# RMSNorm: a one-row store placed between the first and second tile's loads, the third tile in 64 KB rows, gamma in two pieces

## The chip, the cores and the metric

The kernel runs on one core of a Trainium2 chip. Times are device microseconds of that core; unless a span is named, a time is the median of several executions. All executions used here are fast (one core, granted clock 1.0). "Queue" below means the queue of transfers that SyncE issues; every transfer of the kernel is spread over 16 DMA engines, each of which moves its own share.

## The reference

```python
def reference(x, gamma):          # x: 16 x 1024 x 512 float32, gamma: 512 float32
    eps = 1e-5
    rms = np.sqrt(np.mean(x ** 2, axis=-1, keepdims=True) + eps)
    return (x / rms * gamma).astype(np.float32)
```

33.6 MB are read and as many written, with little arithmetic per byte.

## The kernel before

The 16,384 rows form four tiles (t) of 128 partitions x 32 rows x 512 floats: one partition of a tile is 64 KB, contiguous in HBM. Three buffers (slots) hold them; tile 3 reuses the buffer of tile 0. The text says tile 0 to tile 3; the change's own words call tile 2 the third. Rows are handled in groups of 8: ScalarE squares and sums (in every second group VectorE does the summing), VectorE multiplies each row by its 1/rms and by gamma, in place.

```python
    load(0, 0, 0, 8)
    load(0, 0, 8, 16)
    load(0, 0, 16, 32)
    load(1, 1, 0, 32)

    gamma_row = const.tile([1, D], fp32)
    nc.scalar.dma_start(out=gamma_row, in_=gamma.unsqueeze(0))
    # ... gamma is spread over the partitions by a matmul; row_stats and apply are cut

    def transfers(t, g):              # called after apply of tile t, rows g to g+8
        if (t, g) == (0, 0):
            store(0, 0, 0, 1)
            load(2, 2, 0, 16)
            store(0, 0, 1, 2)
            load(2, 2, 16, 24)
            store(0, 0, 2, 3)
            load(2, 2, 24, 32)
        elif (t, g) == (0, 24):
            store(0, 0, 3, 32)
        elif (t, g) == (1, 8):
            store(1, 1, 0, 16)
            load(3, 0, 0, 16)
            load(3, 0, 16, 32)
        # ... stores of tile 1, 2 and 3 in the same way, cut
```

`load(t, slot, r0, r1)` and `store(...)` each issue one transfer of 128 partitions on SyncE, which issues in order and waits for what a transfer needs.

Of the kernel before, what the change touches and what calls it, by code (L numbers as in the profile page):

```python
# [1 line left out]

# [4 lines left out]


@with_exitstack
def kernel(  # L10
    ctx: ExitStack,
    tc: tile.TileContext,
    x: bass.AP,
    gamma: bass.AP,
    out: bass.AP,
):
    nc = tc.nc
    P = nc.NUM_PARTITIONS
    eps = 1e-5
    fp32 = mybir.dt.float32  # L20
    AF = mybir.ActivationFunctionType
    OP = mybir.AluOpType

    xf = x.flatten_outer_dims()
    of = out.flatten_outer_dims()
    N, D = xf.shape
    R = 32
    G = 8
    H = 4
    assert N == 4 * P * R  # L30

    xv = xf.rearrange("(t p r) d -> t p r d", p=P, r=R)
    ov = of.rearrange("(t p r) d -> t p r d", p=P, r=R)

    const = ctx.enter_context(tc.tile_pool(name="const", bufs=1))
    stats = ctx.enter_context(tc.tile_pool(name="stats", bufs=4))
    psum = ctx.enter_context(tc.tile_pool(name="psum", bufs=2, space=bass.MemoryType.PSUM))

    slots = [const.tile([P, R, D], fp32, name=f"slot{i}") for i in range(3)]

    def load(t, slot, r0, r1):
        nc.sync.dma_start(out=slots[slot][:, r0:r1], in_=xv[t][:, r0:r1])

    def store(t, slot, r0, r1):
        nc.sync.dma_start(out=ov[t][:, r0:r1], in_=slots[slot][:, r0:r1])

    load(0, 0, 0, 8)
    load(0, 0, 8, 16)
    load(0, 0, 16, 32)
    load(1, 1, 0, 32)  # L50

    gamma_row = const.tile([1, D], fp32)
    nc.scalar.dma_start(out=gamma_row, in_=gamma.unsqueeze(0))
    ones_col = const.tile([1, P], fp32)
    nc.vector.memset(ones_col, 1.0)  # L55
    gamma_psum = psum.tile([P, H, D], fp32, name="sq")
    nc.tensor.matmul(gamma_psum[:, 0], ones_col, gamma_row, start=True, stop=True)  # L57
    gamma_b = const.tile([P, D], fp32)
    nc.vector.tensor_copy(out=gamma_b, in_=gamma_psum[:, 0])  # L59

    eps_t = const.tile([P, 1], fp32)
    nc.vector.memset(eps_t, eps)  # L62
    sq_scratch = const.tile([P, D], fp32)

    def row_stats(slot, g):
        ss = stats.tile([P, G], fp32, name="ss")
        rms = stats.tile([P, G], fp32, name="rms")
        rstd = stats.tile([P, G], fp32, name="rstd")
        if (g // G) % 2:
            for h in range(0, G, H):  # L70
                sq = psum.tile([P, H, D], fp32, name="sq")
                nc.scalar.activation(out=sq, in_=slots[slot][:, g + h : g + h + H, :], func=AF.Square)  # L72
                nc.vector.tensor_reduce(  # L73
                    out=ss[:, h : h + H], in_=sq, axis=mybir.AxisListType.X, op=OP.add
                )
        else:
            for r in range(G):
                nc.scalar.activation(  # L78
                    out=sq_scratch,
                    in_=slots[slot][:, g + r, :],  # L80
                    func=AF.Square,
                    accum_out=ss[:, r : r + 1],
                )
        nc.scalar.activation(out=rms, in_=ss, func=AF.Sqrt, bias=eps_t, scale=1.0 / D)  # L84
        nc.vector.reciprocal(out=rstd, in_=rms)  # L85
        return rstd

    def apply(slot, g, rstd):
        for r in range(G):
            nc.vector.scalar_tensor_tensor(  # L90
                out=slots[slot][:, g + r, :],
                in0=slots[slot][:, g + r, :],
                scalar=rstd[:, r : r + 1],
                in1=gamma_b,
                op0=OP.mult,
                op1=OP.mult,
            )

    groups = [(t, g) for t in range(4) for g in range(0, R, G)]
    slot_of = [0, 1, 2, 0]  # L100

    def transfers(t, g):
        if (t, g) == (0, 0):
            store(0, 0, 0, 1)
            load(2, 2, 0, 16)
            store(0, 0, 1, 2)
            load(2, 2, 16, 24)
            store(0, 0, 2, 3)
            load(2, 2, 24, 32)
        elif (t, g) == (0, 24):  # L110
            store(0, 0, 3, 32)
        elif (t, g) == (1, 8):
            store(1, 1, 0, 16)
            load(3, 0, 0, 16)
            load(3, 0, 16, 32)
        elif (t, g) == (1, 24):
            store(1, 1, 16, 32)
        elif (t, g) == (2, 24):
            store(2, 2, 0, 32)
        elif (t, g) == (3, 8):  # L120
            store(3, 0, 0, 16)
        elif (t, g) == (3, 24):
            store(3, 0, 16, 32)

    ahead = row_stats(0, 0)
    for k, (t, g) in enumerate(groups):
        rstd = ahead
        if k + 1 < len(groups):
            tn, gn = groups[k + 1]
            ahead = row_stats(slot_of[tn], gn)  # L130
        apply(slot_of[t], g, rstd)
        transfers(t, g)


# [1 line left out]
_INS = ['x', 'gamma']  # L136
_OUTS = [((16, 1024, 512), 'float32')]


# [23 lines left out]
```

## Time and profile before

| | before |
|---|---|
| time, median of the first 3 runs | 162.5 us (162.17 to 163.0) |
| span in the profile | 160.3 us |
| data queue, share of 16 engines' span | 97.8% |
| VectorE / ScalarE busy | 76% / 50% |
| first data packet / last packet on any engine (packet records) | 1.74 / 158.97 us |

From the page of the kernel before: busy time, then the queue (packets, MB, share of 16 engines' span), then the bytes, then the chain of work that ended last, by engine. (PE and PEld are TensorE, DVE is VectorE, ACT ScalarE, POOL GpSimd; SPq marks what SyncE issues, L45 is line 45 of the kernel.)

```profile
span 160.3 us, 415 instructions
PE 2.0 (1%) x2; PEld 0.5 (0%) x2; DVE 122.6 (76%) x163; ACT 80.1 (50%) x162; POOL 0.2 (0%) x4
...
q1 hardware_dynamic: 2592, 67.11, 97.8%
...
HBM read 33.56 MB, written 33.55 MB: 419 GB/s over the span
...
DVE 69%; ACT 12%; DMA 4%; issue 2%; DVEq 0%
```

The queue is full nearly all the time, so the kernel ends when the bytes have passed. Next, SyncE's issues in order of time (start, length, what; a merged line spans several issues and the wait between them).

```profile
0.73 1.89 SPq L42 DMA_DIRECT2D slot<-in_x_dram  x4
20.54 0.35 SPq L45 DMA_DIRECT2D out_dram<-slot  x1
20.93 0.43 SPq L42 DMA_DIRECT2D slot<-in_x_dram  x1
21.41 0.43 SPq L45 DMA_DIRECT2D out_dram<-slot  x1
...
45.84 23.22 SPq L45 DMA_DIRECT2D out_dram<-slot  x2
```

All of tiles 0 and 1 is issued by 2.6 us; when the first small store is issued at 20.54 us, tile 1 still lies ahead of it in the queue, 19 us of work. ScalarE's first instruction on tile 1, with its idle time and what ended it:

```profile
42.16 0.63 ACT L78 ACTIVATE sq_scratch<-slot 128x512 f32<-128x512 f32 x1 [6.91 <-DMA slot<-in_x_dram]
```

### The profile page before, as it was taken

The page shows a single profiled execution, that of the slowest core. Times are in us where ns is not written, and L with a number is a line of the kernel's source. Part 1 is how long each engine was busy: PE and PEld are TensorE (multiplying, and loading weights), DVE is VectorE, ACT ScalarE, POOL GpSimd, SP SyncE. Part 2 cuts the span into 40 slices and gives each one's busy share as a digit, 9 for nine tenths or more (in the row PEclk, how much of TensorE's full clock was granted, in tenths as well). Part 3 has the DMA queues.
Part 4 walks back from the last instruction along what each step waited for, and adds up shares of the span by engine and source line. Part 5 has one row for each costly group of instructions (what it writes and reads, how often), then busy time and mean ns, then how long its engine had stood idle before and what let it go on. Part 6 is the DMA issues. An engine that isn't in the chain of part 4 may idle for free.

```text
span 160.3 us, 415 instructions
## 1 busy us (share of the span) xinstructions
PE 2.0 (1%) x2; PEld 0.5 (0%) x2; DVE 122.6 (76%) x163; ACT 80.1 (50%) x162; POOL 0.2 (0%) x4
## 2 busy tenths in 40 slices
PE   4000000000000000000000000000000000000000
PEld 1000000000000000000000000000000000000000
DVE  0102999999995199999999999999999999950000
ACT  3099739900499999969009600796099400000000
POOL 0000000000000000000000000000000000000000
DMA  6999999969799999998899999999999799799993
GB/s 197 437 413 523 392 392 523 523 262 523 327 403 407 456 435 503 474 444 356 385 441 466 401 409 490 401 401 499 409 515 474 327 507 458 335 392 450 458 401 139
DMA packets 2597, 67.13 MB, mean 419 GB/s; under 512 B 290, under 2 KB 290, under 8 KB 675
## 3 DMA queue, kind: packets, MB, share of 16 engines
q1 hardware_dynamic: 2592, 67.11, 97.8%
q14 instruction: 3, 0.02, 0.0%
q10 hardware_dynamic: 2, 0.00, 0.0%
HBM read 33.56 MB, written 33.55 MB: 419 GB/s over the span
## 4 chain that ended last, share of the span: by engine, by line
DVE 69%; ACT 12%; DMA 4%; issue 2%; DVEq 0%
DVE slot L90 51%; DVE ss L73 17%; ACT sq_scratch L78 7%; ACT sq L72 4%; DMA slot<-in_x_dram 4%; DVE rstd L85 1%; ACT rms L84 1%; DVEq L158 0%
## 5 line engine op out<-in xcount | busy, mean ns | idle before, releaser
L90 DVE SCALAR_TENSOR_TENSOR slot<-slot,rstd,gamma_b 128x512 f32<-128x512 f32 x128 | 85.7, 738 | 0.1
L78 ACT ACTIVATE sq_scratch<-slot 128x512 f32<-128x512 f32 x64 | 40.0, 625 | 16.0 <-DMA slot<-in_x_dram 14.7
L73 DVE TENSOR_REDUCE ss<-sq 128x4 f32<-128x2048 f32 x16 | 36.0, 2274 | 10.1 <-ACT sq L72 10.0
L72 ACT ACTIVATE sq<-slot 128x2048 f32<-128x2048 f32 x16 | 29.8, 1862 | 8.1 <-DVE ss L73 8.1
L84 ACT ACTIVATE rms<-ss,eps_t 128x8 f32<-128x8 f32 x16 | 4.6, 298 | 26.6 <-DVE ss L73 26.4
L78 ACT ACTIVATION_READ_ACCUMULATOR sq_scratch<-slot 128x1 f32 x64 | 11.9, 187 | 0.0
L85 DVE RECIPROCAL rstd<-rms 128x8 f32<-128x8 f32 x16 | 3.1, 192 | 5.7 <-ACT rms L84 5.7
L59 DVE COPY gamma_b<-sq 128x512 f32<-128x512 f32 x1 | 0.7, 692 | 3.2 <-PE sq L57 3.2
L57 PE MATMUL sq<-gamma_row,ones_col 1*128 1x512 f32 x2 | 2.0, 1122 | 2.1 <-DMA gamma_row<-in_gamma_dram 2.1
L78 ACT ACT_TABLE_LOAD x1 | 1.3, 1283 | 1.3 <-PEq L147 1.3
L84 ACT ACT_TABLE_LOAD x1 | 1.3, 1283 | 0.0
L55 DVE MEMSET ones_col<- 1x128 f32 x1 | 0.2, 165 | 0.8 <-PEq L147 0.8
L57 PEld LDWEIGHTS sq<-gamma_row,ones_col 1*128 1x128 f32 x2 | 0.5, 306 | 2.1 <-issue 2.1
L147 POOL MEMSET const-bfloat16-1.0<- 128x1 bf16 x1 | 0.1, 101 | 0.0
L147 POOL MEMSET const-uint8-127<- 128x1 uint8 x1 | 0.1, 101 | 0.0
L147 POOL MEMSET const-float32-0.0<- 128x1 f32 x1 | 0.1, 98 | 0.2 <-issue 0.2
L147 POOL MEMSET const-float32-1.0<- 128x1 f32 x1 | 0.1, 98 | 0.0
L62 DVE MEMSET eps_t<- 128x1 f32 x1 | 0.1, 59 | 0.0
## 6 DMA issues: line engine op xcount, KB each, us to landing
slot<-in_x_dram SPq DMA_DIRECT2D x4, 4096.0 KB, 24.7
out_dram<-slot SPq DMA_DIRECT2D x4, 4096.0 KB, 22.5
slot<-in_x_dram SPq DMA_DIRECT2D x4, 2048.0 KB, 11.5
out_dram<-slot SPq DMA_DIRECT2D x1, 7424.0 KB, 35.8
out_dram<-slot SPq DMA_DIRECT2D x3, 256.0 KB, 32.1
gamma_row<-in_gamma_dram ACTq DMA_DIRECT2D x1, 2.0 KB
slot<-in_x_dram SPq DMA_DIRECT2D x1, 40.0
out_dram<-slot SPq DMA_DIRECT2D x1
```

The lines of the kernel that those rows point to most:

```text
L55: nc.vector.memset(ones_col, 1.0)
L57: nc.tensor.matmul(gamma_psum[:, 0], ones_col, gamma_row, start=True, stop=True)
L59: nc.vector.tensor_copy(out=gamma_b, in_=gamma_psum[:, 0])
L62: nc.vector.memset(eps_t, eps)
L72: nc.scalar.activation(out=sq, in_=slots[slot][:, g + h : g + h + H, :], func=AF.Square)
L73: nc.vector.tensor_reduce(out=ss[:, h : h + H], in_=sq, axis=mybir.AxisListType.X, op=OP.add)
L78: nc.scalar.activation(out=sq_scratch, in_=slots[slot][:, g + r, :], func=AF.Square, accum_out=ss[:, r : r + 1],)
L84: nc.scalar.activation(out=rms, in_=ss, func=AF.Sqrt, bias=eps_t, scale=1.0 / D)
L85: nc.vector.reciprocal(out=rstd, in_=rms)
L90: nc.vector.scalar_tensor_tensor(out=slots[slot][:, g + r, :], in0=slots[slot][:, g + r, :], scalar=rstd[:, r : r + 1], in1=gamma_b, op0=O ...
L147: nc = _bacc.Bacc("TRN2", target_bir_lowering=False, num_devices=1)
```

## The change

The intent: fewer and larger transfers. Two of the three one-row stores go, the third tile (tile 2) is one load with 64 KB per partition instead of three, gamma is loaded in two pieces, and the load of tile 1 moves behind the remaining one-row store.

```diff
     load(0, 0, 16, 32)
-    load(1, 1, 0, 32)
 
     gamma_row = const.tile([1, D], fp32)
-    nc.scalar.dma_start(out=gamma_row, in_=gamma.unsqueeze(0))
+    cuts = [D * i // 2 for i in range(3)]
+    for a, b in zip(cuts, cuts[1:]):
+        nc.scalar.dma_start(out=gamma_row[:, a:b], in_=gamma.unsqueeze(0)[:, a:b])
@@ transfers
             store(0, 0, 0, 1)
-            load(2, 2, 0, 16)
-            store(0, 0, 1, 2)
-            load(2, 2, 16, 24)
-            store(0, 0, 2, 3)
-            load(2, 2, 24, 32)
+            load(1, 1, 0, 32)
+            load(2, 2, 0, 32)
         elif (t, g) == (0, 24):
-            store(0, 0, 3, 32)
+            store(0, 0, 1, 32)
```

## The prediction

> **What bounds the kernel now.** The transfers. The page's queue section gives the data queue 97.8% of 16 engines' span and 419 GB/s; VectorE is busy 76%. In the packet records under that view, from the first data packet (1.74 us) to the last semaphore packet (158.96 us), the 16 engines together are idle for the equal of only about 0.6 us, nearly all at the two ends. The chain of waits names VectorE for 69%, but VectorE finishes at 142.5 us and the last store's packets only come up at 148 us, behind older ones. So a saving counts only if it shortens the queue's work, and a delay costs only if the queue runs dry. The Trainium skill, "DMA: Bandwidth & Descriptors", Bandwidth, gives a ceiling of 435 GB/s; 64 KB packets here took 2.418 us, 27.1 bytes/ns on one engine, 434 GB/s on 16: the trace agrees.
>
> **What the change does to the queue's work.** A packet of 2 KB takes 84 ns, 16 KB 611, 32 KB 1213, 64 KB 2418. Consecutive packets overlap by about 4 ns, so each extra packet costs about 4.7 ns. Per partition, two 2 KB store packets join the large store and the third tile's 32+16+16 KB become one 64 KB: four packets less, 32 per engine, 0.15 us. Four transfers less drop four 9 ns semaphore packets per engine, 0.02 us. Load-to-store turns fall from five to three; the last load packets before a turn ran longer by about 0.34 us at the first store (39 us) and 0.04 to 0.1 us later. Two later ones saved are worth about 0.1 us. Together about 0.25 us.
>
> **What it moves.** The second tile's load is issued behind the first small store. The timeline shows that store issued at 20.54 us, after the first VectorE row; its issue takes about 0.4 us, so the load goes out near 20.95. Tile 0's last packets end between 21.73 and 22.03 us. Issue to first packet took 1.0 us at the kernel's start, so the store's packets are ready near 21.55 us, eight of 80 ns per engine fill until about 22.4 to 22.7, and the load's are ready near 22.0. The queue should just not run dry; slack is 0.2 us for the store, 0.4 us for the load. I allow 0.1 us for a partial gap. Nothing ahead of that row changes order on ScalarE or VectorE.
>
> Tile 1 lands about 0.65 us later (its compute began at 42.16). That is off the path: the large store is issued with some 16 us of queue ahead, tile 1's first store with 11, the last store at 142.5 with 5.6. Tile 2 lands 1 to 2 us earlier, which nobody waits for. Gamma's second issue takes 0.5 us on ScalarE's queue, while ScalarE idles until 7.88.
>
> **Prediction.** 162.5 - 0.25 + 0.1: 162.3 us, range 161.7 to 163.0. Faster by over 2%: 0.01; within 2%: 0.97; slower: 0.02.
>
> **What would show it.** Data packets 2016 against 2592. The one-row store begins between 21.6 and 22.1 us, tile 1's 64 KB packets near 22.5, hardly any idle time around 20 to 24 us; ScalarE's wait for tile 1 ends near 42.8; VectorE ends at 142 to 143.5.
>
> **What would make it wrong.** A longer delay from issue to first packet: every us beyond 1.2 goes straight into the total, as all later transfers wait behind. Or a first row later than 20.5 us. The spread of 0.8 us exceeds the effect.

## The result

| | before | changed |
|---|---|---|
| time, median of 6 runs | 162.45 us (162.17 to 163.0) | 164.94 us (164.4 to 165.26) |
| ratio, 95% interval | | 1.0149 (1.0123 to 1.0174) |
| last packet of the 16 engines (packet records) | 157.82 to 158.97 us | 12 engines 159.36 to 160.22, 4 engines 161.6 to 161.93 us |

Ratios here and below are the mean time of one kernel's fast runs over that of the other's in the same rounds, so not quite the ratio of the medians quoted. By the 2% measure the time is the same; by the interval it is 1.5% slower. 164.94 us lies outside the predicted 161.7 to 163.0.

The page of the changed kernel, the same parts, and the first line of its chain that ended last:

```profile
span 163.1 us, 408 instructions
PE 2.0 (1%) x2; PEld 0.5 (0%) x2; DVE 122.8 (75%) x163; ACT 80.0 (49%) x162; POOL 0.2 (0%) x4
...
q1 hardware_dynamic: 2016, 67.11, 96.9%
...
HBM read 33.56 MB, written 33.55 MB: 411 GB/s over the span
...
DVE 52%; DMA 19%; ACT 15%; issue 2%; DVEq 0%; SPq 0%
```

Packets fell exactly as counted ahead, from 2592 to 2016, and still the queue's share fell and the span grew. The part of DMA in the chain went from 4% to 19%. SyncE's issues:

```profile
0.73 1.33 SPq L42 DMA_DIRECT2D slot<-in_x_dram  x3
20.75 0.35 SPq L45 DMA_DIRECT2D out_dram<-slot  x1
21.14 0.94 SPq L42 DMA_DIRECT2D slot<-in_x_dram  x2
46.06 25.92 SPq L45 DMA_DIRECT2D out_dram<-slot  x2
```

and ScalarE's first instruction on tile 1:

```profile
45.52 0.63 ACT L79 ACTIVATE sq_scratch<-slot 128x512 f32<-128x512 f32 x1 [10.06 <-DMA slot<-in_x_dram]
```

In the chain that ended last (start, length, what) of the changed kernel, tile 1's load now stands by itself:

```profile
20.64 0.21 DVE rstd L86
20.85 0.25 SPq L45
21.10 0.04 issue
21.14 24.36 DMA slot<-in_x_dram
45.50 0.02 issue
```

Tile 1 is issued at 21.14 us, as foreseen to 0.2 us, and ScalarE gets it at 45.52 us, where 42.8 was predicted. A 64 KB row takes 2.418 us on its engine and each engine carries eight, 19.3 us. So 24.36 us from issue to landing leaves about 5 us for something else. The records of single packets show what:

```
tile 1's first 64 KB packet on each of the 16 engines, start in us (changed kernel)
22.69 22.79 22.98 22.99 23.00 23.05 23.06 23.07 23.09 23.12 23.14 23.18 | 24.59 24.71 24.90 25.14
end of tile 0's last packets: 21.61 to 22.24; one-row store's packets: from 21.79 to 23.18
```

Twelve engines pass from the store to tile 1 without a gap. Four finish the store among the first, at 22.70 to 22.89 us, find nothing, and stand idle for about 2 us. (The records do not name the engine; which packets follow each other is read from their times. On the twelve a 64 KB packet starts within 6 ns of the end of the store's last semaphore packet, the 4-byte packet by which an engine reports its share done; on the four none does.) In addition the packets are slower around this place: the store's 2 KB packets took up to 204 ns instead of 84, and the first two 64 KB packets of an engine up to 3.35 us instead of 2.418. The four engines stay behind the others to the end: they finish tile 1 at 44.7 to 45.2 us while the others finish at 42.9 to 43.5, and close the kernel 1.4 to 2.6 us after them. Each engine has a fixed share of the partitions, so the others cannot help. The Trainium skill, "DMA: Bandwidth & Descriptors", The descriptor swizzle, gives that fixed assignment; this trace is consistent with it, though its records name no engine: in tile 1's load and in all nine later transfers the group of four ends at least 1.1 us after the slowest of the twelve.

Three quantities per engine describe the loss (averages over 16 engines, worked out from the packet records: idle from 20 to 30 us; stretch, that is packet time above the usual 84, 611, 1213, 2418 ns of its size, or above size over 27.1 bytes/ns for other sizes):

| | before | changed |
|---|---|---|
| idle, 20 to 30 us | 0.00 us | 0.62 us (about 2 us on four engines) |
| stretch, 20 to 30 us | 0.01 us | 0.98 us |
| stretch, 30 to 56 us | 0.37 us | 0.05 us |
| stretch, 56 to 66 us (turn to the large store of tile 0) | 0.15 us | 1.08 us |
| median engine's last packet | 158.05 us | 159.86 us |

The median engine loses 1.8 us, mostly by stretch; the last engine, which ends the kernel, loses about 3 us in this pair of profiles.

### The profile page after: what moved, and what is told of

Same layout as the page of the kernel before. It is cut to its first block, busy times and chain, and to the rows that moved or that the text cites. A ratio compares the mean times of both kernels' runs of the same rounds, so it can differ in the third digit from the quotient of the medians.

```text
span 163.1 us, 408 instructions
## 1 busy us (share of the span) xinstructions
PE 2.0 (1%) x2; PEld 0.5 (0%) x2; DVE 122.8 (75%) x163; ACT 80.0 (49%) x162; POOL 0.2 (0%) x4
## 3 DMA queue, kind: packets, MB, share of 16 engines
q1 hardware_dynamic: 2016, 67.11, 96.9%
## 4 chain that ended last, share of the span: by engine, by line
DVE 52%; DMA 19%; ACT 15%; issue 2%; DVEq 0%; SPq 0%
DVE slot L91 38%; DMA slot<-in_x_dram 19%; DVE ss L74 13%; ACT sq_scratch L79 8%; ACT sq L73 6%; DVE rstd L86 1%; ACT rms L85 0%; DVEq L156 0%; SPq L45 0%
```

## The experiments

The first four were to settle which part of the change costs. Theory D: the queue runs dry because tile 1's load comes too late. Rivals: G, the second gamma piece; P, 64 KB packets next to a turn between loading and storing.

**a1_gamma_one**, gamma in one piece again.

```diff
-    cuts = [D * i // 2 for i in range(3)]
-    for a, b in zip(cuts, cuts[1:]):
-        nc.scalar.dma_start(out=gamma_row[:, a:b], in_=gamma.unsqueeze(0)[:, a:b])
+    nc.scalar.dma_start(out=gamma_row, in_=gamma.unsqueeze(0))
```

> Undoes gamma in two pieces, all else as changed. Theory D (the queue runs dry when the second tile's load is issued only behind the one-row store): unchanged, 164.9 us +-0.5, four or more engines again start tile 1's 64 KB packets about 2 us after their last store packet. Rival G (the second gamma piece, which landed only at 6.5 us, disturbs the start): back to 162.3 to 162.7 us.

Measured: 165.12 us (before on the same chip 162.65), ratio 1.0155 (1.0129 to 1.0182). Three engines start tile 1 late, at 23.8, 24.0 and 24.7 us. D had said four or more. G falls: gamma is not it.

**a2_load1_first**, tile 1 loaded up front again, all else changed.

```diff
     load(0, 0, 16, 32)
+    load(1, 1, 0, 32)
@@ transfers
             store(0, 0, 0, 1)
-            load(1, 1, 0, 32)
             load(2, 2, 0, 32)
```

> Undoes the late load alone: tile 1's load issued up front as before, then one one-row store, tile 3's rows of 64 KB, gamma in two. Theory D: the late engines vanish; 162.2 to 163.3 us, since one cost is left, the stretched 64 KB packets of tile 2 at the turn to the large store (0.97 us per engine after, against about 0.5 us for all turns of before). Rival P (64 KB packets next to a turn between loads and stores are the main cost, not the late load): stays at 164.0 or above. Rival G: stays near 164.9.

Measured: 162.24 us against 162.65, ratio 0.9972 (0.9955 to 0.9988). No idle time from 20 to 30 us. Its span is 160.7 us, and its first instruction on tile 1 is back where it was in the kernel before:

```profile
42.14 0.63 ACT L80 ACTIVATE sq_scratch<-slot 128x512 f32<-128x512 f32 x1 [6.74 <-DMA slot<-in_x_dram]
```

D holds: putting this one load back takes the whole loss away, and what is left of the change is a small gain. P as the main cost falls.

**a3_tile2_halves**, the third tile in two loads of 32 KB rows.

```diff
-            load(2, 2, 0, 32)
+            load(2, 2, 0, 16)
+            load(2, 2, 16, 32)
```

> As changed, but the third tile in two loads of 32 KB rows. Theory D says the late start is the same, so at least 163.8 us. Rival P, for the second stretch: the last packets of tile 2 before the large store near 61 us lose their stretch (from 0.97 us mean per engine to under 0.2 us) and the time falls by 0.6 to 0.9 us, to about 164.1. If packet size does not matter at the turn: 164.9 and the stretch stays near 1 us in total.

Measured: 165.21 us, ratio 1.0161 (1.0135 to 1.0187); the stretch from 56 to 66 us is 1.12 us, as with 64 KB rows (1.08). P falls for the second stretch too: the row size is not its cause.

**a4_quarter_first**, eight rows of tile 1 up front, the rest behind the store.

```diff
     load(0, 0, 16, 32)
+    load(1, 1, 0, 8)
@@ transfers
             store(0, 0, 0, 1)
-            load(1, 1, 0, 32)
+            load(1, 1, 8, 32)
```

> As changed, but 8 rows of tile 1 (4.9 us of queue) are loaded up front and 24 rows after the one-row store, so the queue is not dry when the store and the load come. Theory D: no engine idles near 22 to 25 us, time 162.3 to 163.5 us. Rival (it is the place of the store between loads, not the dry queue): stays near 164.5 or above.

Measured: 162.29 us, ratio 0.9975 (0.9960 to 0.9990), idle from 20 to 30 us 0.01 us. The store may stand between loads; the queue only must not be nearly empty then. This settles the first question.

The second question is why a load issued 0.5 to 1.1 us before tile 0's last packets end, with 0.65 us of store packets besides, comes too late. Theory L: under load the way from issue to first packet is long on some engines. Rival R: an engine that once finds its queue empty takes 2 us to restart. Rival S: the turn from load to small store and back costs. Later B: the small store just ahead delays the load. The next kernels vary the lead. Where a load is to be held back without a store, one column of its buffer is first written by VectorE from a finished row; the load overwrites it, so results stay correct.

**b1_cushion1**, one row of tile 1 (0.65 us of queue) up front; **b2_cushion2**, two rows; **e1_cushion4**, four rows.

```diff
     load(0, 0, 16, 32)
+    load(1, 1, 0, n)          # n = 1, 2, 4
@@ transfers
-            load(1, 1, 0, 32)
+            load(1, 1, n, 32)
```

> As changed, but one row of tile 1 (8 packets, about 0.65 us of queue per engine) is loaded up front. Theory L (a load issued while the queue is busy reaches some engines only up to 4 us after its issue, whatever they do meanwhile): the late engines still start tile 1's large packets near 24 to 25 us, idle about 1.3 us instead of 2, so 163.7 to 164.6 us. Theory R (a queue found empty for even a moment takes 2 us to restart): the descriptors are in time and no engine is late, 162.2 to 162.8 us.

> The same with two rows up front (about 1.3 us of queue). Theory L: late engines idle about 0.7 us, 163.0 to 163.8 us, between the one-row cushion and none. Theory R: 162.2 to 162.8 us, the same as the one-row cushion.

> As changed, with four rows of tile 1 (about 2.4 us of queue per engine) loaded up front. Theory L: the worst start seen was 4.0 us after the issue, 2.0 us after the queue ran dry, so 2.4 us of lead just covers it: no late engine, 162.2 to 162.7 us, level with eight rows (162.29) and clearly under two rows (163.07). If eight rows were needed for another reason: 162.8 or more.

Measured, with the two ends of the series (stretch and idle from each one's profile):

| rows of tile 1 up front | time | ratio to before | idle 20-30 us | stretch 20-30 / 56-66 us |
|---|---|---|---|---|
| 0 (changed) | 164.94 | 1.0149 | 0.62 | 0.98 / 1.08 |
| 1 | 164.09 | 1.0104 | 0.18 | 0.30 / 1.34 |
| 2 | 163.07 | 1.0036 | 0.05 | 0.48 / 0.33 |
| 4 | 161.83 | 0.9973 | 0.02 | 0.33 / 0.91 |
| 8 | 162.29 | 0.9975 | 0.01 | 0.28 / 0.70 |
| 32 (a2_load1_first) | 162.24 | 0.9972 | 0.00 | 0.00 / 0.55 |

The medians come from several sets of runs, so compare the ratios. (The 161.83 us with four rows is below the 162.2 to 162.7 expected, on a chip on which the kernel before was at 162.31.) The instruction of ScalarE that waited for the rest of tile 1, with one, two and four rows in front:

```profile
44.29 0.63 ACT L80 ACTIVATE sq_scratch<-slot 128x512 f32<-128x512 f32 x1 [8.92 <-DMA slot<-in_x_dram]
```

```profile
43.27 0.63 ACT L80 ACTIVATE sq_scratch<-slot 128x512 f32<-128x512 f32 x1 [7.33 <-DMA slot<-in_x_dram]
```

```profile
42.86 0.63 ACT L80 ACTIVATE sq_scratch<-slot 128x512 f32<-128x512 f32 x1 [5.43 <-DMA slot<-in_x_dram]
```

The time falls row by row and is level from four rows on, 2.4 us of lead. Counted from the issue of the rest of tile 1 to its first packet, the work ahead was 1.9 us with one row, 2.8 with two and 4.2 with four; only the last exceeds the 4.0 us that the slowest engine of the changed kernel took. R, which wanted one row to suffice, falls. L had the times of one and two rows right, but its picture of the engines was not. With one row a single engine stands out, 3.20 us after the issue where the others start within 2.66. For two rows it foresaw late engines idle for 0.7 us, and the profile shows 0.05 us of idle time on average and 0.48 us of stretch. These two profiles are not typical of their kernels either: the one-row profile is its slowest run (164.97 us), the two-row profile its fastest (162.69).

**b3_held_row7**, the loads held until eight rows are multiplied, so that the queue is truly empty.

```diff
     def apply(...):           # for the first group only, after row 7
+                for s in (1, 2):
+                    nc.vector.tensor_copy(out=slots[s][:, 0, 0:1], in_=slots[0][:, g + r, 0:1])
```

> As changed, but tile 1's and tile 2's loads are held until the eighth row is multiplied (a one-column copy into their buffers, overwritten by the load), so they are issued near 25.6 us into a queue that has been empty since about 23. If the latency is long only under load (L), all 16 engines start tile 1 between 26.6 and 27.3 us, 1.0 to 1.6 us after the issue as at the start of the kernel, with no late group, and the time is about 4.2 us over the version with the load up front: 166 to 167 us. If restarting an empty queue costs 2 us or more (R), starts lie at 27.6 us or later and the time is 167.3 or more.

Measured: 168.06 us, ratio 1.0348 (1.0321 to 1.0375). SyncE's issues:

```profile
20.62 0.35 SPq L45 DMA_DIRECT2D out_dram<-slot  x1
26.05 0.80 SPq L42 DMA_DIRECT2D slot<-in_x_dram  x2
```

and the queue's line of its page, 94.7% where the changed kernel had 96.9%:

```profile
q1 hardware_dynamic: 2016, 67.11, 94.7%
```

All 16 engines start tile 1 between 27.02 and 27.35 us, 0.97 to 1.30 us after the issue. So an empty queue restarts in about 1 us on every engine, and R falls a second time. But the time is 168.06, above L's 166 to 167: beyond 4.5 us of idle, the first packets after the empty time are stretched by 0.77 us per engine, and those near the turn to the large store by 1.03. L had no term for that. It is to be seen at the kernel's own start: there the packets that start before 2.0 us took 0.53 us longer per engine than later ones in the profile of before, and 0.25 to 0.58 us in the others.

**c1_held_nostore**, no small store, the loads held to the same moment as in the changed kernel.

```diff
+                for s in (1, 2):       # after row 0 of the first group
+                    nc.vector.tensor_copy(out=slots[s][:, 0, 0:1], in_=slots[0][:, g + r, 0:1])
@@ transfers
-            store(0, 0, 0, 1)
             load(1, 1, 0, 32)
             load(2, 2, 0, 32)
         elif (t, g) == (0, 24):
-            store(0, 0, 1, 32)
+            store(0, 0, 0, 32)
```

> No one-row store at all; tile 1's and tile 2's loads are held to about the same moment (the first row multiplied, 20.9 us) by a one-column copy. L or R: some engines still start tile 1 late, idle 2 us or more since there is no store to bridge, 164.5 to 166 us. Rival S (the turn from a load to a small store and back is what costs): no late engine, 162.3 to 163 us.

Measured: 164.13 us, ratio 1.0109 (1.0078 to 1.0140). The issue:

```profile
20.80 0.80 SPq L42 DMA_DIRECT2D slot<-in_x_dram  x2
```

Tile 1 starts 1.15 to 1.96 us after its issue at 20.80 us. Both expectations miss in part: no group of engines starts 2 us after the rest, as S said, yet the time is nowhere near 162.3 to 163. The loss here is 0.38 us of idle and 0.76 plus 1.23 us of stretch. A load issued as the queue runs out costs without any store in front of it; the store makes the worst engine later still.

**c2_all_held**, the one-row store too is held (row 0 is multiplied last of its eight), then the loads, all into an empty queue.

```diff
-        for r in range(G):
+        for r in [*range(1, G), 0] if first else range(G):
@@ and the same one-column copies after row 0
```

> Row 0 is multiplied last of its eight, so the one-row store is issued near 25.5 us and the loads near 26.2 us, both into an empty queue. If it is the busy queue that makes the second issue late (L): all engines start tile 1's packets within 1.6 us of the load's issue, as in the held run without a store in front (0.97 to 1.30 us), time within 0.5 us of that run's 168.06. If it is the small store just ahead (B, descriptors of a transfer are made only after those of the one before): some engines start 2 to 4 us after the issue, a late group is there at the end, and the time is 169 us or more.

Measured: 168.39 us, ratio 1.0348 (1.0331 to 1.0364). The issues:

```profile
25.45 0.35 SPq L45 DMA_DIRECT2D out_dram<-slot  x1
26.18 0.82 SPq L42 DMA_DIRECT2D slot<-in_x_dram  x2
```

The store's first packets come 0.85 us after its issue at 25.45 us; tile 1's, issued at 26.18 us, 0.99 to 1.36 us after on thirteen engines, and 1.81, 1.82 and 2.10 us after on three. Between the two expectations: the store ahead delays a few engines by up to 0.8 us even when the queue is empty (some of B), but not to the 4 us of the changed kernel, and the time is within 0.5 us of the previous held run (L).

**c3_store_on_act**, the one-row store issued from ScalarE's queue, the loads held to the same moment as in c1_held_nostore.

```diff
-            store(0, 0, 0, 1)
+            nc.scalar.dma_start(out=ov[0][:, 0:1], in_=slots[0][:, 0:1])
@@ and the same one-column copies after row 0
```

> As changed, with the one-row store issued from ScalarE's queue and the loads held to the same moment on the other. B says the two still hinder each other: late engines (2 us or more after the issue), 164.3 to 165.2. If only the order within one queue matters: load starts as in the held run without a store (1.2 to 2.0 us after issue) and 163.8 to 164.3 us. No version of this is expected to beat the kernel before.

Measured: 164.06 us, ratio 1.0087 (1.0062 to 1.0111). Tile 1 starts 1.13 to 2.66 us after its issue at 20.85 us. In time it is level with the held run without a store; two engines, at 2.07 and 2.66 us, are later than any there (1.96). The other queue mends nothing, and it does not keep the two apart: on thirteen engines one 2 KB packet of the store now passes per 64 KB packet of tile 1, so that the store's packets, done by 23.2 us in the changed kernel, end only at 38.5 us. This kernel is therefore not a clean test of B.

Start of tile 1's large packets after its issue, first and last engine, over all these runs:

| run | queue at the issue | store issued just ahead | first / last engine |
|---|---|---|---|
| b3_held_row7 | empty | no | 0.97 / 1.30 us |
| c2_all_held | empty but for the store | yes | 0.99 / 2.10 us |
| c1_held_nostore | busy to about 1 us after | no | 1.15 / 1.96 us |
| c3_store_on_act | the same | on the other queue | 1.13 / 2.66 us |
| changed, and its repeat | the same | yes | 1.55 / 4.00, 1.45 / 3.69 us |
| a1_gamma_one, a3_tile2_halves | the same | yes | 1.54 / 3.64, 1.63 / 3.59 us |

(The first engine's value is bounded from below by the packets ahead of it; the last engine's, where it was idle before, is the delay itself.)

Two more asked about the stretch of packets near 59 us, at the turn to the first large store.

**d1_no_small_store**: all three tiles up front, no small store.

```diff
     load(0, 0, 16, 32)
+    load(1, 1, 0, 32)
+    load(2, 2, 0, 32)
@@ transfers
-            store(0, 0, 0, 1)
-            load(1, 1, 0, 32)
-            load(2, 2, 0, 32)
+            pass
         elif (t, g) == (0, 24):
-            store(0, 0, 1, 32)
+            store(0, 0, 0, 32)
```

> No small store, all three tiles loaded up front, one store of 64 KB rows. No engine late. If the stretch of the last load packets at the first large store (0.5 us mean per engine with one small store ahead, 0.1 with three) is a cost of the first stores that small ones pay in advance, it is now 0.8 to 1.2 us, and the time is 162.2 to 162.8; if the stretch belongs to each turn alone, one turn less saves 0.3 us and 8 packets per engine: 161.8 to 162.1.

Measured: 162.52 us, ratio 0.9982 (0.9966 to 0.9999); stretch from 56 to 66 us 1.17 us and nothing elsewhere.

**d2_first_split**: tile 1 up front, one small store, tile 2 in 32+16+16 KB rows.

```diff
     load(0, 0, 16, 32)
+    load(1, 1, 0, 32)
@@ transfers
             store(0, 0, 0, 1)
-            load(1, 1, 0, 32)
-            load(2, 2, 0, 32)
+            load(2, 2, 0, 16)
+            load(2, 2, 16, 24)
+            load(2, 2, 24, 32)
```

> Tile 1 up front, one one-row store, tile 2 in 32+16+16 KB rows as before: the kernel before without its second and third small store. If the rows of 64 KB make the turn to the large store cost 0.5 us instead of 0.1: faster than with tile 2 whole, about 161.9 to 162.1 us. If it is the missing small stores that do it: the stretch stays near 0.5 us and the time is 162.2 to 162.5.

Measured: 162.16 us, ratio 0.9980 (0.9946 to 1.0014), between the two expected times; stretch 0.29 us at the small store and 0.48 us at the large one. With a full queue the two turns together thus stretch by about 0.5 us with three small stores (before), 0.8 to 0.9 with one, 1.2 with none. That fits a cost of the first stores which small ones pay in part in advance, and not one of row size. It is not more than a fit: there is one profile for each of the cases with three and with none, that of d1_no_small_store is its slowest run (163.5 us, the other four took 162.22 to 162.56), and the runs of d2_first_split scatter from 161.87 to 163.1. In the runs whose queue ran dry it is 1.0 to 1.5 us at the large store although in all but c1_held_nostore a small store came before; why is open.

Last, the changed kernel and the better version once more, five rounds on one chip, with e1_cushion4 above.

**e2_changed_again**: the changed kernel, no edit.

> The changed kernel itself, on the same chip as the others, for a second profile. L: again some engines (one to six, not necessarily four) start tile 1 over 1 us late and stay behind the rest to the end; 164.5 to 165.3 us. If the late group of the first profile was an accident of that one run, it is absent here and the time is under 164.

Measured: 165.0 us against 162.31, ratio 1.0161 (1.0136 to 1.0186). Five engines start tile 1 late, from 23.92 to 24.75 us, and end last, at 161.0 to 162.36 us. The late group belongs to the kernel; how many engines are in it changes from run to run.

**e3_load1_first_again**: the edit of a2_load1_first.

> The version with tile 1's load up front again, five rounds, to see whether it really beats the kernel before: 162.0 to 162.4 us, ratio 0.996 to 0.999 with an interval under 1. No late engine.

Measured: 161.94 us, ratio 0.9984 (0.9959 to 1.0009). The interval just includes 1; that of the first measurement (0.9955 to 0.9988) and those of the versions with four and eight rows up front do not. So the gain is about 0.2 to 0.3%. The version with four rows up front had the lowest median, 161.83 us against 162.31 for before on the same chip.

## Why the prediction was wrong

- **What bounds the kernel: right.** All runs fit a time set by when the queue is filled and how fast its packets go; VectorE and ScalarE, late by 3 us in the changed kernel, never made it wait. The last store was issued near 145.5 us, while older packets filled the engines until 149.7 us or later.
- **The saving: right in size, by its terms not shown.** The packet count was exact (2016). With tile 1 up front the same saving measured 0.16% and 0.28%, 0.26 and 0.46 us, where 0.25 us was predicted. But 0.1 us of this was to come from fewer turns, and the stretch at the turns grew, from 0.5 us before to 0.8 to 0.9 with one small store; that the sum came out may be luck.
- **Gamma: right.** Its second piece landed at 6.5 us and VectorE copied gamma at 9.02 instead of 4.23 us, still well before 20 us; undoing it changed nothing. It held a warning, though it came only with the changed kernel: its issue on ScalarE's queue was over at 1.49 us and its packet started at 5.81, 4.3 us later, while the loads filled the queue (in the other profiles with two pieces 5.33 to 5.76 us). In the profiles with gamma in one piece the packet started at 1.6 us.
- **The issue times: right.** Store 20.75 (predicted 20.54), load 21.14 (20.95), first store packet 21.79 us (21.6 to 22.1).
- **The step that failed** is this one: "Issue to first packet took 1.0 us at the kernel's start, so the store's packets are ready near 21.55 us [...] and the load's are ready near 22.0. The queue should just not run dry". The 1.0 us was the first packet on the first engine, into an empty queue (the sixteenth engine's first packet came 1.44 us after the issue in the same records). The load's packets have to be ready on all 16 engines, and here they were so only 3.6 to 4.0 us after the issue on the slowest. The last engine ends the kernel. The allowance of 0.1 us stood against some 2 us of idle time on three to five engines.
- **A term that was missing:** packets just after the queue has run low or dry are slow, 0.63 to 0.98 us per engine in all eight profiles of kernels that load no row of tile 1 ahead of the wait. The kernel's start already showed about 0.5 us of it. The further 1.0 to 1.5 us at the turn to the large store was not foreseen either: the prediction counted turns, three against five, and called them worth 0.1 us.
- **What would make it wrong: named rightly, weighed wrongly.** "A longer delay from issue to first packet" was the cause. A range of 1.3 us and a chance of 2% for over 2% did not reflect that the slack was 0.2 to 0.4 us and the delay had been measured once, in other conditions.

What is shown: tile 1's late issue causes the loss (undone alone, the loss is gone); it acts through idle engines and stretched packets; about 2.4 us of loads ahead is enough. What stays open: why the delay differs between engines, what exactly the small store ahead adds in a busy queue, and what stretches the packets at the large store in the runs that ran dry.

## What to carry to other kernels

When the queue of transfers is the limit, do not let the next load's issue hang on a computed result unless the queue still holds more work than the slowest engine's delay. Here that delay was up to 4.0 us; 4.2 us of work from the issue on (four rows of loads, 2.4 us, with the rest of tile 0 and the store) was enough, and 2.8 us (two rows) still cost 0.36%. Judge a delay by the slowest of the 16 engines and under the load it will meet, not by the first packet at the start of the kernel. The Trainium skill's rule to issue a DMA early and wait on its semaphore late ("DMA: Bandwidth & Descriptors", Rules for kernel authors) is borne out: the same transfers with one load moved back up front took 162.24 instead of 164.94 us.

## What the Trainium skill lacked or had wrong

- "DMA: Bandwidth & Descriptors", Latency and other measured facts, gives about 600 ns to the first byte on this path. An empty queue agrees on the first engines: 0.97 to 1.30 us from the issue's start, some 0.6 to 0.9 us from its end (an issue takes about 0.4 us). For a queue that is busy, with another transfer issued just ahead, it gives no such figure: 3.6 to 4.0 us on the slowest engine here.
- The same page, Why a DMA increments its semaphore by 16 and not by 1, says that a DMA's engines finish independently, but not what follows for a chain of transfers: engines that fall behind once stay behind. Three to five of 16, which started tile 1 0.6 to 2.0 us after the slowest of the others, were still 0.8 to 1.4 us behind the slowest of the others at 160 us and set the time.
- No page has the slow first packets into an empty queue: about 0.5 us per engine at the kernel's start, 0.6 to 1.0 us after a dry moment (a 64 KB packet up to 3.35 us instead of 2.418).
- No page has the slow last load packets ahead of the first stores: 0.3 to 0.4 us per engine ahead of the first small store, 0.15 to 1.5 us ahead of the first large one.
- "DMA: Bandwidth & Descriptors", Rules for kernel authors, asks for 1 MiB or more per DMA but does not say how little smaller ones lose while the queue is full: two stores of 256 KB and two splits of a load less gave only 0.2 to 0.3% here.
